# Convolution, projections and attention of a hybrid encoder layer recorded with interleaved priorities, the convolution writing the mix first

## The chip, the cores and the metric

One Trainium2 chip (trn2), all 8 NeuronCores, one launch. Each core handles one new stream of 2048 frames and two running streams of 64 frames; weights are read by every core. The time is device microseconds of the slowest core. Some executions of these kernels fall into a slower state, in which the cores of one die show a lower granted clock (in the changed kernel's one of 2205.4 us, cores 0 to 3 have 0.84 to 0.85, the others 0.97 to 0.98); those runs are left out of every comparison here.

## The reference, cut to what matters

```python
def encoder_layer(x, c, ...):
    x = x + 0.5 * gt1 * swiglu(modulate(rmsnorm(x)), w_ffn1_in, w_ffn1_out)
    h = modulate(rmsnorm(x, g_mix), sh2, sc2)
    z = h @ w_in                                   # q k v f | B C X | gate_attn gate_conv
    logf = log_sigmoid(z_f + b_f)
    o_attn = fox_attention(q, k, v, logf, past_k, past_v, past_logf)   # 16 heads of 64
    o_conv = z_B * short_conv(z_C * z_X, past_u, conv_w)
    m = sigmoid(z_GA) * o_attn + sigmoid(z_GC) * o_conv
    x = x + gt2 * (m @ w_out)
    x = x + 0.5 * gt3 * swiglu(modulate(rmsnorm(x)), w_ffn2_in, w_ffn2_out)
```

Attention and convolution both read `h` and meet only in `m`. Nothing in the reference says which is computed first, nor which of them writes `m` and which adds.

## The kernel before

The kernel records every operation as a node with its buffers and a **priority** (a lower number goes first). A list scheduler inside the program builder then fixes, ahead of time, the order of the instructions on each engine and the slots of the tile pools; semaphores follow from that order. Head pairs are numbered `c` = 0 to 7, position blocks `tb` = 0 to 3 (512 frames) and 4 (the running streams).

```python
p_a = Pool("a", banks[0:4], excl=True)        # PSUM: scores (and FFN)
p_o = Pool("o", banks[4:6], excl=True)        # attention output, output projection
p_p = Pool("p", banks[6:8], excl=True)        # PSUM: projections
...
LOOK = -0.008                                  # scores go ahead of their turn by this
def attend(c):
    ...                                        # per q block, head, key tile of 128:
    mm(scores -> p_a tile, prio=LOOK)          # 1 matmul of up to 512 columns (+ mask)
    act(exp: p_a tile -> pt tile)              # ScalarE, bias from the forget sums
    mm(pt x v -> p_o tile)                     # up to 4 matmuls of 65 columns
    ...
    # gate: t2 * (1 + tanh), transpose through p_p, then
    copy(lambda: (mv(c, tb), pt.ap[:, 0:n // 2].bitcast(BF16)), n, [pt], [MB[c][tb]])   # WRITES the mix
def conv(c):
    for tb, (t0, n) in enumerate(TBS):
        gate = conv_end[-2:-1]                 # wait for the convolution two blocks back
        pc = proj(wC, tb, None, gate); px = proj(wX, tb, None, gate)
        ...                                    # u = C * X; three taps on VectorE (line 1260, 1264)
        pb = proj(wB, tb, None, gate)          # cy = B * cy          (line 1269)
        pg = proj(wG, tb, None, gate)          # cy = cy * (1 + tanh) (line 1274)
        conv_end.append(dve(mv(c, tb) = cy + mv(c, tb)))   # ADDS to the mix (line 1277)
...
for c in range(8):
    P.at(300.0 + c * 10 + 5);  kvqga(c + 1)    # keys, queries, values, attention gate
    P.at(300.0 + c * 10);      attend(c)
    P.at(500.0 + c * 10);      conv(c)         # after everything else of the sub-layer
...
# output projection: residual loads wait for the last convolution
P.dma("sync", xo <- xs, [XS[tb]], [xo], [lastc])
```

`pb` in the profiles is PSUM; `RG`, `RX`, `SC` are SBUF regions, `WS` the weights, `H` the normalised input. So `pb<-H,WS` are projections and feed-forward matmuls, `pb<-WS,H` the projections with positions as rows, `RG<-pb,NF` the exponentials.

The softmax here doesn't subtract the row's maximum and nothing guards it: scores larger than these inputs give would overflow.

Of the kernel before, what the change touches and what calls it, by code (L numbers as in the profile page):

```python
# [15 lines left out]
NT = 2176  # L16
NPR = 2048
# [96 lines left out]
class Node:  # L114
    __slots__ = ("idx", "alts", "deps", "outs", "prio", "dma", "alloc", "tiles", "ndep",
                 "ready", "eng", "start", "fin", "tok", "need", "know", "tbl", "done", "q")


class Prog:
# [19 lines left out]

    def _new(self, reads, writes, after, prio):  # L140
# [11 lines left out]
        n.prio = self.base + self.step * 1e-3 + (prio or 0.0)  # L152
# [243 lines left out]
    def assign(self):  # L396
# [38 lines left out]
        while did < total:  # L435
# [36 lines left out]
            if not moved:  # L472
                for e, o in self.order.items():
                    if ptr[e] < len(o):
                        n = o[ptr[e]]
                        print([(t.pool.name, [m.idx for m in t.nodes]) for t in n.tiles], n.ndep)
                        print(e, ptr[e], n.idx, n.start, n.ready, [(m.idx, m.eng, m.start, m.fin, k) for m, k in n.deps.items() if id(m) not in ready])
# [39 lines left out]
def build_program():  # L517
# [34 lines left out]
    with ExitStack() as ctx:  # L552
# [51 lines left out]
        p_a = Pool("a", banks[0:4], excl=True)  # L604
        p_o = Pool("o", banks[4:6], excl=True)
        p_p = Pool("p", banks[6:8], excl=True)
# [339 lines left out]
        def rgf(off, n):  # L946
# [3 lines left out]
        T1F = rx(BOFF[0], NT)  # L950
        CT16 = rxb(BOFF[0] + 8704, NT)
        ETF = rx(BOFF[1], NT)
        B_t1f, B_ct, B_etf = Buf("t1f", xu[0]), Buf("ct", xu[0]), Buf("etf", xu[1])
        B_ctd = Buf("ctd")

        k_augs = [rg(GB_[0], 2 * NT).rearrange("p (h t) -> p h t", h=2),
                  rxb(BOFF[0], 2 * NT).rearrange("p (h t) -> p h t", h=2)]
        q_augs = [rg(GB_[1], 2 * NT).rearrange("p (h t) -> p h t", h=2),
                  rxb(BOFF[1], 2 * NT).rearrange("p (h t) -> p h t", h=2)]
        VW = 17 * 2 * 66  # L960
        v_exts = [rg(GB_[2], VW).rearrange("p (i h d) -> p i h d", i=17, h=2),
                  rxb(BOFF[0] + 8704, VW).rearrange("p (i h d) -> p i h d", i=17, h=2)]
# [13 lines left out]
        sl_b0 = Slot(rx(BOFF[0] + 13192 + 8, 512), xu[0])  # L976
        sl_b1 = Slot(rx(BOFF[1] + 12928, 512), xu[1])
        a_b0 = Slot(rxb(BOFF[0] + 13192 + 8 + 2048, 512), xu[0])
        a_b1 = Slot(rxb(BOFF[1] + 12928 + 2048, 512), xu[1])
        sl_b4 = [Slot(rx(BOFF[4], 512), xu[4]), Slot(rx(BOFF[4] + 2048, 512), xu[4])]  # L980
        sl_g3 = Slot(rgf(GB_[3] + 8192, 512), gu[3])
        p_sga = Pool("sga", [sl_b0, sl_b1, sslots[0], sslots[1]])
# [6 lines left out]
        p_at = Pool("at", [a_b0, a_b1])  # L989
# [21 lines left out]
        for (o, n, init) in ((0, NPR, None), (NPR, SQ, 0), (NPR + SQ, SQ, 1)):  # L1011
# [12 lines left out]
        fu = B_t1f.users() + B_ct.users()  # L1024
        eu = B_etf.users()
        B_k = [[[Buf("k", gu[0]) for _ in range(5)] for _ in range(2)],
               [[Buf("k", xu[0] + fu) for _ in range(5)] for _ in range(2)]]
        B_krow = [Buf("krow", gu[0]), Buf("krow", xu[0] + fu)]
        B_q = [[[Buf("q", gu[1]) for _ in range(5)] for _ in range(2)],
               [[Buf("q", xu[1] + eu) for _ in range(5)] for _ in range(2)]]  # L1030
        B_qrow = [[Buf("qrow", gu[1]) for _ in range(2)], [Buf("qrow", xu[1] + eu) for _ in range(2)]]
        B_v = [[Buf("v", gu[2]) for _ in range(5)], [Buf("v", xu[0] + fu) for _ in range(5)]]
        B_vone = [Buf("vone", gu[2]), Buf("vone", xu[0] + fu)]
# [34 lines left out]
        sga = {}  # L1068

        def kvqga(c):  # L1070
# [11 lines left out]
            for tb, (t0, n) in enumerate(TBS):  # L1082
# [10 lines left out]
                for hh in range(2):  # L1093
# [14 lines left out]
                sgt = p_sga.tile()  # L1108
                pg, _ = proj_tok(wG, tb, (), [sgt])
                sga[(c, tb)] = sgt  # L1110
                act(lambda sgt=sgt, pg=pg, nt=nt: (sgt.ap[:, 0:nt * 128], pg.ap[:, 0:nt * 128]), AF.Tanh,
                    nt * 128, [pg], [sgt], scale=0.5)
# [7 lines left out]
        LOOK = -0.008  # L1120

        def attend(c):
# [15 lines left out]
            def gate(tb, nsub, t2):  # L1138
                n = nsub * 128
                sgt = sga[(c, tb)]  # L1140
                at = p_at.tile()
                dve(lambda e: e.scalar_tensor_tensor(out=at.ap[:, 0:n], in0=sgt.ap[:, 0:n], scalar=1.0,
                                                     in1=t2.ap[:, 0:n], op0=ALU.add, op1=ALU.mult),
                    n, [sgt, t2], [at])
                pt = p_p.tile()
                tr(lambda: [(pt.ap[:, s * 64:(s + 1) * 64].bitcast(BF16), at.ap[:, s * 128:(s + 1) * 128],
                             ident_bf[:]) for s in range(nsub)], [at, B_const], [pt], [128] * nsub)
                copy(lambda: (mv(c, tb), pt.ap[:, 0:n // 2].bitcast(BF16)), n, [pt], [MB[c][tb]], rate=1.5)

            for qb in range(4):  # L1150
                q0 = qb * 512
                t2 = p_t2.tile()
                for hh in range(2):
# [3 lines left out]
                    for i in range(nt):  # L1157
                        r = i - 4 * qb
                        lo = max(r, 0) * 128
                        s_ = p_a.tile()  # L1160
# [18 lines left out]
                gate(qb, 4, t2)  # L1179

            t2 = p_t2.tile()
            for hh in range(2):
                head = 2 * c + hh
                ot = p_o.tile()
                s_ = p_a.tile()
                mm(lambda s_=s_, hh=hh: [
                    (s_.ap[:, 0:128], ka[0:65, hh, NPR:NT], qa[0:65, hh, NPR:NT], True, False),
                    (s_.ap[:, 0:128], ident_bf[:], mask2[:], False, True)],
                   [B_k[st][hh][4], B_krow[st], B_q[st][hh][4], B_qrow[st][hh], B_const], [s_], [128, 128],
                   prio=LOOK)  # L1190
                pt = p_pt.tile()
                act(lambda pt=pt, s_=s_: (pt.ap[:, 0:128], s_.ap[:, 0:128]), AF.Exp, 128, [s_, B_nf], [pt],
                    bias=NF[:, 256 + head:257 + head], scale=1.0)
                mm(lambda pt=pt, ot=ot, hh=hh: [(ot.ap[:, 0:65], pt.ap[:, 0:128], va[:, 16, hh, 0:65], True, False)],
                   [pt, B_v[st][4], B_vone[st]], [ot], [65], nogroup=True)
                for s in range(2):
                    s_ = p_a.tile()
                    c0 = NPR + s * SQ
                    mm(lambda s_=s_, s=s, hh=hh, c0=c0: [
                        (s_.ap[:, i * 64:(i + 1) * 64], kc_aug[0:65, s, hh, i * 128:(i + 1) * 128],  # L1200
                         qa[0:65, hh, c0:c0 + SQ], True, True) for i in range(8)],
                       [B_kc, B_kcrow, B_q[st][hh][4], B_qrow[st][hh]], [s_], [64] * 8, prio=LOOK)
                    bt = p_t2.tile()
                    dve(lambda e, s_=s_, bt=bt, s=s, head=head: e.tensor_tensor(
                        out=bt.ap[:, 0:512].rearrange("p (i q) -> p i q", i=8),
                        in0=s_.ap[:, 0:512].rearrange("p (i q) -> p i q", i=8),
                        in1=NFS[:, s * 128:(s + 1) * 128].rearrange("p (i h) -> p i h", i=8)[
                            :, :, head:head + 1].to_broadcast([128, 8, 64]), op=ALU.add),
                        512, [s_, B_nfs], [bt])
                    pt = p_pt.tile()  # L1210
                    act(lambda pt=pt, bt=bt: (pt.ap[:, 0:512], bt.ap[:, 0:512]), AF.Exp, 512, [bt], [pt])
                    mm(lambda pt=pt, ot=ot, s=s, hh=hh: [
                        (ot.ap[s * 64:(s + 1) * 64, 0:65], pt.ap[:, i * 64:(i + 1) * 64],
                         vc_ext[:, s, i, hh, 0:65], False, s == 1 and i == 7) for i in range(8)],
                       [pt, B_vc], [ot], [65] * 8, nogroup=True)
                finish(ot, 1, hh, t2)
            gate(4, 1, t2)
# [4 lines left out]
        def conv(c):  # L1222
# [6 lines left out]
            for tb, (t0, n) in enumerate(TBS):  # L1229
                sg = segs(tb)  # L1230
                gate = conv_end[-2:-1]
                pc = proj(wC, tb, None, gate)
                t1 = p_t1.tile()
                copy(lambda t1=t1, pc=pc, n=n: (t1.ap[:, 0:n], pc.ap[:, 0:n]), n, [pc], [t1])
                px = proj(wX, tb, None, gate)
# [31 lines left out]
                pb = proj(wB, tb, None, gate)  # L1267
                for si, (lo, ln_, seq) in enumerate(sg):
# [3 lines left out]
                pg = proj(wG, tb, None, gate)  # L1272
                act(lambda pg=pg, n=n: (pg.ap[:, 0:n], pg.ap[:, 0:n]), AF.Tanh, n, [], [pg], scale=0.5)
                dve(lambda e, pg=pg, cy=cy, n=n: e.scalar_tensor_tensor(
                    out=cy.ap[:, 0:n], in0=pg.ap[:, 0:n], scalar=1.0, in1=cy.ap[:, 0:n],
                    op0=ALU.add, op1=ALU.mult), n, [pg, cy], [cy])
                conv_end.append(dve(lambda e, cy=cy, tb=tb, n=n: e.tensor_tensor(
                    out=mv(c, tb), in0=cy.ap[:, 0:n], in1=mv(c, tb), op=ALU.add), n, [cy, MB[c][tb]], [MB[c][tb]]))

        P.at(300.0)  # L1280
        cache_load(0)
        kvqga(0)
        for c in range(8):
            if c + 1 < 8:
                P.at(300.0 + c * 10 + 5)
                kvqga(c + 1)
            P.at(300.0 + c * 10)
            attend(c)
            if c + 1 < 8:
                P.at(300.0 + c * 10 + 6)  # L1290
# [192 lines left out]
```

## Time and profile before

| | before |
|---|---|
| fast runs, us | 2178.0, 2179.3, 2184.8 (slow state: 2299.6) |
| spans of the cores in the profiled run | 2160.6 to 2179.7 |
| TensorE / ScalarE (ACT) / VectorE (DVE) busy | 89% / 35% / 38% |
| first score matmul to last product with values (core 7) | 667 to 1258 us |
| convolution alone after that | to about 1541 us |

The prediction shows the main lines. One more view belongs with them: the chain that ended last, in order of time, in one position block of the convolution (start, length, what; the small pieces left out).

```profile
1347.63 3.63 PE pb L646 x16
...
1351.42 0.70 DVE RG L1238
...
1353.15 0.76 DVE SC L1264
1354.00 0.76 DVE SC L1264
...
1354.92 0.70 DVE SC L1269
...
1355.76 3.63 PE pb L646 x16
```

From one pair of projections to the next, 8.1 us pass. TensorE is the chain for 3.63 us, VectorE's taps and products for the rest, in part beside TensorE's other pair: with two projection banks, the next projection can't start until line 1269 has read one of them. The profile puts 45.8 us of TensorE's waits from 1268 to 1541 us to that line, in 35 waits (core 0).

### The profile page before, as it was taken

How to read it: one execution, taken by the hardware profiler on the slowest of the kernel's cores; microseconds unless marked ns; L12 is line 12 of the kernel's file. 1: busy time of each engine (PE TensorE's matmuls, PEld its weight loads, DVE VectorE, ACT ScalarE, POOL GpSimd, SP SyncE). 2: the span in 40 equal slices, each digit the busy share in tenths (PEclk: the TensorE clock that was granted, in tenths of full speed). 3: DMA queues.
4: the chain of work that ended last, by engine and by line, in shares of the span. 5: the costliest groups of instructions: out<-in, count | busy, mean ns of one | idle time of the engine just before them, and what ended most of it. 6: DMA issues, size and time to landing. Idle time of an engine off the chain costs nothing.

```text
span 2179.7 us, 38451 instructions; the slowest of 8 cores (2160.6 to 2179.7 us)
## 1 busy us (share of the span) xinstructions
PE 1949.7 (89%) x14273; PEld 1052.6 (48%) x14273; DVE 837.1 (38%) x1592; ACT 755.4 (35%) x1425; POOL 163.1 (7%) x312
## 2 busy tenths in 40 slices
PE   2599999999879999999998988788789999999986
PEld 0245445544336666666666643333334444444433
DVE  0432232223444334433533356666545122322244
ACT  3621101113435576577567630000047110011122
POOL 2101102110011000000000000000000000010000
PEclk7699999999877899999999999999999999999998
DMA  9924506552262222221322211111153221042022
GB/s 237 142 43 68 89 1 95 83 85 64 88 115 63 50 51 64 62 55 48 82 51 53 62 20 20 32 28 20 27 139 78 49 39 20 1 86 36 15 77 87
DMA packets 67460, 137.50 MB, mean 63 GB/s; under 512 B 8416, under 2 KB 12640, under 8 KB 65728
## 3 DMA queue, kind: packets, MB, share of 16 engines
q0 software_dynamic: 41680, 80.92, 23.1%
q1 hardware_dynamic: 25600, 54.12, 7.3%
q8 instruction: 119, 1.95, 0.4%
q14 instruction: 61, 0.50, 0.1%
HBM read 180.04 MB, written 35.89 MB: 99 GB/s over the span
## 4 chain that ended last, share of the span: by engine, by line
PE 74%; DVE 10%; issue 6%; ACT 5%; DMA 4%; DVEq 0%; SPq 0%; ACTq 0%; POOLq 0%; POOL 0%
PE pb L646 74%; ACT RG L668 4%; DVE SC L1264 2%; DMA G<-g 1%; DVE SC L1269 1%; DVE RG L1238 1%; DVE SC L798 1%; ACT H L668 1%; ACT SC L668 1%; DMA BADA<-b_ada 1%; DVE SC L1260 1%; DVE SC L812 1%; DMA WS<-w_ada 0%; DMA yT<-SC 0%; DVE RX L853 0%
## 5 line engine op out<-in xcount | busy, mean ns | idle before, releaser
L646 PE MATMUL pb<-H,WS 128*128 128x512 bf16 (+2 forms) x5480 | 1059.2, 352 | 69.0 <-DVE SC L1269 47.8
L646 PEld LDWEIGHTS pb<-H,WS 128*128 128x128 bf16 (+1 forms) x5480 | 489.4, 99 | 599.9 <-issue 124.6
L646 PE MATMUL pb<-RG,WS 128*128 128x512 bf16 (+1 forms) x1888 | 366.6, 355 | 33.7 <-DVE RX L853 31.3
L668 ACT ACTIVATE SC<-pb 128x512 bf16<-128x512 f32 (+3 forms) x260 | 138.4, 533 | 716.8 <-PE pb L646 710.0
L668 ACT ACTIVATE RG<-pb,NF 128x512 bf16<-128x512 f32 (+3 forms) x656 | 338.6, 792 | 13.0 <-PE pb L646 12.4
L837 DVE TENSOR_TENSOR RG<-pb,SC 128x512 bf16<-128x512 f32 (+1 forms) x220 | 134.5, 612 | 478.0 <-PE pb L646 463.7
L646 PEld LDWEIGHTS pb<-RG,WS 128*128 128x128 bf16 x1888 | 174.6, 101 | 223.4 <-issue 65.3
L853 DVE SCALAR_TENSOR_TENSOR RX<-pb,DER,RX 128x512 f32<-128x512 f32 (+1 forms) x192 | 112.8, 595 | 232.8 <-PE pb L646 229.7
L646 PE MATMUL pb<-RG 128*128 128x65 bf16 (+4 forms) x1424 | 148.5, 236 | 15.8 <-ACT RG L668 4.8
L668 ACT ACTIVATE SC<-RX 128x512 bf16<-128x512 f32 (+1 forms) x160 | 84.8, 559 | 187.0 <-PE pb L646 89.6
L646 PE MATMUL pb<-WS,H 128*128 128x128 bf16 x2176 | 132.9, 222 | 5.3 <-DVE RG L680 4.1
L646 PE MATMUL pb<-RX 65*128 65x512 bf16 (+3 forms) x456 | 116.9, 317 | 18.0 <-ACT RG L668 4.9
L646 PEld LDWEIGHTS pb<-WS,H 128*128 128x128 bf16 x2176 | 126.3, 100 | 13.2 <-issue 11.6
L646 PEld LDWEIGHTS pb<-RG 128*128 128x128 bf16 (+1 forms) x1424 | 87.2, 101 | 66.0 <-issue 42.6
L668 ACT ACTIVATE pb<-pb 128x512 f32<-128x512 f32 (+1 forms) x40 | 20.7, 518 | 268.2 <-PE pb L646 268.2
L646 PE MATMUL pb<-RX,RG 128*128 128x65 bf16 (+1 forms) x1352 | 98.5, 199 | 1.1 <-ACT RG L668 0.8
L646 PEld LDWEIGHTS pb<-RX,RG 128*128 128x128 bf16 (+1 forms) x1352 | 79.4, 104 | 32.2 <-issue 9.4
L668 ACT ACTIVATE H<-SC,MOD 128x512 bf16<-128x512 f32 (+1 forms) x144 | 78.4, 591 | 47.7 <-DVE SC L798 47.6
L798 DVE SCALAR_TENSOR_TENSOR SC<-RX,DER,SC 128x512 f32<-128x512 f32 (+1 forms) x144 | 78.8, 593 | 26.5 <-ACT H L668 18.1
L1128 DVE RECIPROCAL RS<-pb 128x4 f32<-128x4 f32 (+1 forms) x80 | 14.2, 178 | 162.7 <-PE pb L646 161.5
L646 PE MATMUL pb<-SC,ones_bf 128*128 128x512 bf16 (+1 forms) x160 | 50.1, 387 | 29.1 <-ACT SC L668 29.0
L693 POOL DMA_DIRECT2D WS<-w_in x64 | 33.8, 540 | 491.4 <-PE pb L646 488.9
(100 smaller groups left out, 1037.3 us busy)
## 6 DMA issues: line engine op xcount, KB each, us to landing
WS<-w_ada POOLq DMA_DIRECT2D x72, 256.0 KB, 9.9
WS<-w_in POOLq DMA_DIRECT2D x64, 256.0 KB, 5.8
WS<-w1i POOLq DMA_DIRECT2D x44, 256.0 KB, 9.2
WS<-w2i POOLq DMA_DIRECT2D x44, 256.0 KB, 7.3
RX<-xT SPq DMA_DIRECT2D x4, 2048.0 KB
xs<-RX SPq DMA_DIRECT2D x4, 2048.0 KB
kT<-SC SPq DMA_DIRECT2D x32, 256.0 KB
vo<-SC SPq DMA_DIRECT2D x32, 256.0 KB
```

The lines of the kernel that those rows point to most:

```text
L646: ins = e.matmul(o, lhsT=l, rhs=r, start=st, stop=sp, skip_group_check=nogroup)
L668: return e.activation(out=out, in_=in_, func=func, **kw)
L693: P.dma("gpsimd", lambda e: e.dma_start(out=t.ap[:, 0:n], in_=src), 128 * n * 4, (), [t], after, prio)
L798: dve(lambda e, k=k, tm=tm, lo=lo, ln_=ln_, seq=seq: e.scalar_tensor_tensor(out=tm.ap[:, lo:lo + ln_], in0=xap(k, tb, lo, ln_), scalar=der ...
L812: dve(lambda e, k=k, tm=tm: e.scalar_tensor_tensor(out=tm.ap[:, 0:n], in0=xap(k, tb), scalar=g3v[:, 3, k, 0:1], in1=rs.ap[:, 0:n], op0=ALU ...
L837: dve(lambda e, n=n, tb=tb, jj=jj, sa=sa, pb=pb: e.tensor_tensor(out=gap(jj, tb), in0=pb.ap[:, 0:n], in1=sa.ap[:, 0:n // 2].bitcast(BF16), ...
L853: dve(lambda e, tb=tb, mo=mo, po=po, lo=lo, ln_=ln_, seq=seq: e.scalar_tensor_tensor(out=xap(mo, tb, lo, ln_), in0=po.ap[:, lo:lo + ln_], ...
L1128: dve(lambda e: e.reciprocal(out=rc.ap[:, 0:nsub], in_=ot.ap[:, 0:nsub * 66].rearrange("p (s d) -> p s d", s=nsub)[:, :, 64]), nsub, [ot], ...
L1238: dve(lambda e, u=u, px=px, t1=t1, lo=lo, ln_=ln_, si=si: e.tensor_tensor(out=u.ap[:, lo + 2 + 2 * si:lo + 2 + 2 * si + ln_], in0=px.ap[:, ...
L1260: dve(lambda e, u=u, cy=cy, m=m: e.tensor_scalar(out=cy.ap[:, 0:m], in0=u.ap[:, 0:m], scalar1=CW[:, c * 3:c * 3 + 1], scalar2=None, op0=AL ...
L1264: dve(lambda e, u=u, cy=cy, m=m, j=j: e.scalar_tensor_tensor(out=cy.ap[:, 0:m], in0=u.ap[:, j:j + m], scalar=CW[:, c * 3 + j:c * 3 + j + 1 ...
L1269: dve(lambda e, pb=pb, cy=cy, lo=lo, ln_=ln_, si=si: e.tensor_tensor(out=cy.ap[:, lo:lo + ln_], in0=pb.ap[:, lo:lo + ln_], in1=cy.ap[:, lo ...
```

## The change

Its intent: let the convolution run beside attention, so that TensorE always has projections to do while ScalarE works on exponentials. For that the convolution writes the mix and attention adds to it; the gate projection of attention moves into attention; priorities are spread over each piece in proportion to its TensorE time. Cut to its core:

```diff
+    def spread(self, first, lo, hi):           # priorities by TensorE share
+        ns = self.nodes[first:]
+        tot = sum(n.alts["tensor"][1] for n in ns if "tensor" in n.alts) or 1.0
+        acc = 0.0
+        for n in ns:
+            n.prio = lo + (hi - lo) * acc / tot + n.extra
+            if "tensor" in n.alts:
+                acc += n.alts["tensor"][1]
...
+        p_s = Pool("s", banks[0:3], excl=True)            # scores: 3 banks for 4
-        p_p = Pool("p", banks[6:8], excl=True)
+        p_p = Pool("p", [banks[3]] + banks[6:8], excl=True)   # projections: 3 for 2
...
-        LOOK = -0.008
+        LOOK = -0.03
...          attention's gate
-                copy(lambda: (mv(c, tb), pt...bitcast(BF16)), n, [pt], [MB[c][tb]], rate=1.5)
+                dve(lambda e: e.tensor_tensor(out=mv(c, tb), in0=pt..., in1=mv(c, tb), op=ALU.add), ...)
...          convolution: no `gate`, and one VectorE operation less
-                dve(... cy = (pg + 1) * cy ...)
-                conv_end.append(dve(... mv(c, tb) = cy + mv(c, tb) ...))
+                conv_end.append(dve(... mv(c, tb) = (pg + 1) * cy ...))
...          order
-            P.at(300.0 + c * 10 + 5); kvqga(c + 1)
-            P.at(300.0 + c * 10);     attend(c)
-            P.at(500.0 + c * 10);     conv(c)
+            lastk = spread(kvq, c, V0 + c - 1.0, V0 + c - 0.1)
+            spread(conv, c, V0 + c - 0.75, V0 + c + 0.2)
+            spread(attend, c, V0 + c, V0 + c + 1)          # gate projection inside
...          output projection: residual loads
-                    128 * n * 4, [XS[tb]], [xo], [lastc])
+                    128 * n * 4, [XS[tb]], [xo], [lastk])
```

Left out: the sample streams' attention moves to the middle of `attend`, the first head pair's buffers change places with the second's, two small pools fall away, the residual loads have three buffers for four. `LOOK` counts in other units in the two kernels (single steps of the recording before, shares of a head pair's work after), so its two values can't be compared directly.

## The prediction

> **What bounds the kernel now.** I read the spans of the eight cores first: 2160.6 to 2179.7 us in the profiled execution, so no core is an outlier, and the two fast timed runs are 2179.3 and 2184.8 (the third, 2299.6, is the slow state). Then the page of the slowest core:
>
> ```profile
> PE 1949.7 (89%) x14273; PEld 1052.6 (48%) x14273; DVE 837.1 (38%) x1592; ACT 755.4 (35%) x1425; POOL 163.1 (7%) x312
> PE   2599999999879999999998988788789999999986
> ACT  3621101113435576577567630000047110011122
> PEclk7699999999877899999999999999999999999998
> ```
>
> TensorE looks 89% busy, but ends of matmuls are modelled, so that row hides waits. The ACT row is the telling one: high for slices 12 to 24, zero for slices 25 to 29. Two halves of the mixing sub-layer stand one after the other: attention (much ACT) and then the convolution (no ACT). I cut the span at these borders and asked for each stretch:
>
> ```profile
> core 0: us, PE busy (x) PEld busy (x) DVE busy (x) ACT busy (x) POOL busy (x), PEclk, DMA share, GB/s
> 540.00:650.00 110.00, 87.09 (x397) 39.16 (x395) 49.66 (x93) 44.62 (x83) 7.59 (x15) 0.79 0.42 97
> 650.00:1268.00 618.00, 570.82 (x6594) 392.16 (x6593) 244.84 (x494) 412.47 (x793) 28.30 (x49) 0.94 0.25 57
> 1268.00:1541.00 273.00, 222.47 (x1137) 100.90 (x1135) 179.79 (x374) 21.25 (x44) 12.67 (x24) 0.97 0.14 24
> 1541.00:1672.00 131.00, 110.75 (x566) 51.63 (x566) 73.66 (x129) 58.62 (x94) 5.19 (x10) 0.96 0.31 85
> 1672.00:2090.00 418.00, 417.40 (x2254) 202.39 (x2255) 104.45 (x182) 71.43 (x142) 29.68 (x57) 1.00 0.22 37
> ```
>
> The last row is a feed-forward stretch and gives the yardstick. Its matmuls are 1804 of 512 columns and 440 of 128, which start 216 and 56 ns apart: 1804 x 0.216 + 440 x 0.056 = 414 of 418 us. So dense TensorE work loses 1%. The same count (starts read from the trace, 65-column matmuls 30 ns apart, 384 and 256 columns 162 and 109) for the others:
> - 650 to 1268, attention with projections: 2176 x 0.056 + 514 x 0.216 = 233 for projections; 448 x 0.216 + 64 x 0.162 + 64 x 0.109 = 114 for scores, 2192 x 0.030 = 66 for weights times values, some 52 for masks, transposes and the cached streams. Sum 465 of 618 us: 153 lost.
> - 1268 to 1541, convolution: 904 x 0.216 + 224 x 0.056 = 208 of 273: 65 lost.
> - 1541 to 1672, output projection: 106 at these spacings, 25 lost. 540 to 650: 83, 27 lost.
>
> What the waits are:
>
> ```profile
> 854.67 16.23 ACT L668 ACTIVATE RG<-pb,NF 128x512 bf16<-128x512 f32 x30
> ```
> ```profile
> L668 ACT ACTIVATE RG<-pb,NF 128x512 bf16<-128x512 f32 x448 | 273.7, 879 | 2.4 <-PE pb L646 1.8
> ```
> ```profile
> PE pb L646 <- DVE SC L1269: 45.8, 35, 2.5
> ```
> ```profile
> 1355.76 6.42 PE L646 MATMUL pb<-H,WS 128*128 128x512 bf16 x29 [1.07 <-DVE SC L1269]
> ```
>
> First line, ACT in the last third of one head pair's attention: 30 exponentials back to back, no gap, 0.54 us each (a full one starts 0.57 after the last). TensorE's share of a full tile is 0.216 + 4 x 0.030 = 0.34 us. With no other matmuls left at that point, ACT is the bound. Second: one exponential lasts 0.88 us from start to end[...]. Third and fourth, from the convolution: TensorE waits some 1 us per position block, 35 times, for the VectorE product that frees a PSUM bank.
>
> [...]cores 0 and 1 record 0.8125 from about 575 to 735 us, the other six do not[...].
>
> **The change part by part.**
> 1. *Removed:* the convolution's last add into the mix. 32 x 0.692 + 8 x 0.293 = 24 us of DVE. The gate's copy out of PSUM (24 DVE at 0.425, some on ACT at 0.58, small ones) becomes an add: 24 us for 17. DVE and ACT together save about 17 us, in stretches where neither is full: nothing directly. What counts is the order: the convolution no longer waits for attention's result, so it can run before it.
> 2. *Moved:* the order of the built program shows it. Cut into pieces of 25 us of TensorE work, the old order has pieces with 21 us of projections, then pieces with 22 us of attention, then eight pieces of convolution alone. The new one has, from the first score tile on, about 7.7 attention, 8.6 convolution, 8.7 projections in every piece for 600 us. No matmul is added: both programs hold the same TensorE work.
> 3. *Distance:* TensorE work between a score matmul and the product that needs its exponential: median 1.24 us before, 2.73 after; 347 of 688 products have less than the needed 1.25 before, 67 after, most at the end of the last head pair.
> 4. *Banks:* scores keep 3 banks of 4, projections get 3 for 2. Three score tiles per 1.4 us round trip is 0.47 us each, shorter than an exponential: no bound.
> 5. *ACT in the mix:* exponentials 448 x 0.569 + 64 x 0.463 + 64 x 0.356 + 80 x 0.25 = 327, cached streams 17, tanh 36, and copies (97 now on ACT by the new order, 69 before) about 43: 423 us in some 700, 60%. DVE about 390, 56%. Both below TensorE.
> 6. *Ends:* the first head's convolution fills the wait for the cumulative forget sums (chain at 656 to 665 us), worth a few us; the residual loads of the output projection no longer wait for the convolution, worth perhaps 5. The last head pair has no projections and soon no convolution beside it: 20 us of exponentials against 11 of TensorE, about 10 us lost.
>
> Sum for 650 to 1541 (891 us): floor 465 + 208 = 673. Attention's loss scaled by the short distances, 153 x 67/347 = 30. For the convolution's bank waits I take a quarter of 65, 16: a third bank and other matmuls between. That is 719, a gain of 172. Ends: some 3 more. 2184.8 - 175 = 2010.
>
> **The rivals.**
> - *ACT or DVE order becomes the wait.* The order on each engine is fixed ahead of time[...]. For: twice as many switches of kind (2380 runs of equal matmuls against 1947), 79 projection copies now among the exponentials, one score bank less. Against: 1.5 us slack over the need, and the old stretches that have projections beside attention are already dense. If half of the old loss stays: 891 - 110 gives about 2075.
> - *The clock.* If 1500 us without rest bring the 0.8125 of cores 0 and 1 back, for example over 300 us, that costs 300 x (1/0.8125 - 1) = 69: about 2080. For: it appeared right after 464 dense us. Against: six cores did not have it, and 440 to 505 dense us in the second feed-forward part have it nowhere.
> - *All of it gained*, [...]floor 2184.8 - (153 + 65 + 20) = 1947. Cores' clock of 0.94 in attention speaks for some of it.
> - *Weight loads late*, since gate weights are held through attention: eight slots hold two sets, and DMA is at 25%; I give it little.
>
> **Range and chances.** 2010; the first two rivals together set the upper end at 2085, the third the lower at 1955. Even half the gain is over 5%, so faster by 2%: 0.95; within: 0.04; slower: 0.01.
>
> **What would show it.** Right: the ACT row at 5 to 7 through the whole mixing stage and no slices of zero; the stage from the first score to the last product about 700 us long; no run of exponentials without gaps except in its last 30 us; TensorE waits for L1269's successor a few us. The prediction is wrong if TensorE waits in the mix for exponentials or bank readers add to over 100 us, if the clock row falls to 8 there, or if the gain of the middle is given back in the output projection.

Its sum: 673 + 30 + 16 = 719 of 891 us, a gain of 172, with 3 for the ends 175, so 2184.8 - 175 = 2010. "The needed 1.25" is the time in us from the end of a score matmul's issue to the product with its exponential; it was partly the author's estimate, and the 30 rests on it. The trace of core 7 before gives nearly the same: 0.20 from the end of a score matmul's issue to the exponential's start and 0.14 from its end to the product (medians of waits) make 1.22 with the 0.88, and 1.44, the "round trip", with the 0.216 of the matmul itself. That the busy row hides waits can be read from the records: one of 512 columns lasts 387 to 394 ns on core 0, and dense ones start 216 ns apart. In the first rival, that late VectorE copies hold TensorE had no measurement behind it. In the third, the 20 us in the floor were the author's estimate for half-speed spells; the clock records before do show such spells, but not what sets them off.

## The result, and the profile after

The changed kernel took 1982.7, 1983.7 and 1985.3 us in its fast runs (one slow run of 2205.4), median of all four 1984.5; before, 2182.0. The ratio is 0.910, with a 95% interval of 0.907 to 0.912. Ratios here and below are the mean time of one kernel's fast runs over that of the other's of the same rounds, so not quite the ratio of the medians quoted. Executions in which one die ran at a lower clock are left out of the means. Results are correct. Later the same two kernels gave 1985.2 and 2175.3, 0.913.

The page of the slowest core after (busy times, then 40 equal slices of the span in tenths):

```profile
PE 1850.1 (93%) x14273; PEld 1012.9 (51%) x14273; DVE 783.5 (39%) x1524; ACT 794.9 (40%) x1455; POOL 163.1 (8%) x312
PE   2499999999987999999999999998999999999986
ACT  3541100111343366666666766668573110111122
PEclk9999999999997999999999999998999999999998
```

The ACT row no longer has a hole: it is at 6 or more from slice 15 on and falls only where attention ends. The clock row stays at 9 through the whole mix. The stretches, cut at the new borders, with the same columns as before:

```profile
650.00:695.00 45.00, 40.55 (x286) 21.89 (x284) 28.17 (x39) 10.38 (x20) 5.45 (x6) 0.92 0.27 61
695.00:1325.00 630.00, 623.15 (x6855) 402.06 (x6854) 338.04 (x739) 409.82 (x755) 35.01 (x66) 1.00 0.31 61
1325.00:1389.00 64.00, 57.03 (x672) 38.87 (x668) 20.53 (x57) 49.03 (x93) 4.76 (x9) 0.92 0.30 51
1389.00:1480.00 91.00, 87.10 (x449) 41.27 (x450) 52.33 (x87) 55.09 (x88) 0.95 (x2) 0.98 0.32 90
1480.00:1895.00 415.00, 414.61 (x2249) 201.22 (x2248) 106.16 (x186) 75.62 (x145) 29.67 (x57) 1.00 0.25 38
```

The second row is the mix: 630 us with a granted clock of 1.00 on all eight cores, and TensorE shown busy but for 7 us. The list of what TensorE waited for there, in all (us, times, longest):

```profile
PE pb L657 <- ACT SC L679: 2.7, 14, 0.4
PE pb L657 <- ACT RG L679: 1.6, 7, 0.5
```

This list shows only a part: the record of a 512-column matmul lasts 0.38 us on average here (core 7), and dense ones start 0.216 apart, so the records cover waits. In the old attention, where the prediction counts 153 us lost, its largest entry for TensorE was no more than this (core 0, 650 to 1268 us):

```profile
PE pb L646 <- ACT RG L668: 10.7, 49, 0.5
```

Counted by the starts of matmuls, as below, the 630 us lose 22, not 4. Some 19 of these lie in steps over 60 ns longer than the dense spacing; the semaphores put 5 of them to exponentials, 5 to copies on ACT, 2 to VectorE, and for 7 they name nobody. By the same count the old attention of core 7 lost 145 us, of which 84 are put to exponentials.

And ACT in the last head pair's attention, where nothing is left to mix in:

```profile
1369.58 16.84 ACT L679 ACTIVATE RG<-pb,NF 128x512 bf16<-128x512 f32 x31
```

This is the old picture, 31 exponentials without a gap, once instead of eight times.

To say where the time came from, I count matmuls times their dense spacing in each stretch, as in the prediction, and call the rest lost. Core 7 has a complete record in both traces and no stretch at 0.8125 of the clock:

| core 7, from 650 us on | before: us (lost) | after: us (lost) |
|---|---|---|
| to the first score matmul | 17 (6) | 45 (9) |
| first score to last product | 591 (146) | 693 (43.5) |
| from there to the end | 912 (123) | 596 (37) |
| - of which convolution alone | (65) | none |
| - output projection, to dense feed-forward | (30) | (6) |
| - the rest, mostly the final norm | (28) | (31) |
| sum lost | 275 | 90 |

The difference, some 186 us, is that of the two spans (2170.5 and 1983.8). The count is good to about 1 us per stretch, depending on the spacing taken for the smallest matmuls. Of the 43.5 us, 22 lie in the mix and 21 in the last 64 us, where attention stands alone. Below, "the mix" in such counts is the whole stretch from the first score to the last product.

### The profile page after: what moved, and what is told of

It reads as the page before. It is cut to its first block, busy times and chain, and to the rows that moved or that the text cites. A ratio compares the mean times of both kernels' runs of the same rounds, so it can differ in the third digit from the quotient of the medians.

```text
span 1983.8 us, 38303 instructions; the slowest of 8 cores (1978.3 to 1983.8 us)
## 1 busy us (share of the span) xinstructions
PE 1850.1 (93%) x14273; PEld 1012.9 (51%) x14273; DVE 783.5 (39%) x1524; ACT 794.9 (40%) x1455; POOL 163.1 (8%) x312
## 4 chain that ended last, share of the span: by engine, by line
PE 86%; DMA 4%; DVE 4%; issue 3%; ACT 3%; POOL 0%; DVEq 0%; SPq 0%; ACTq 0%; POOLq 0%
PE pb L657 85%; DMA WS<-w_ada 3%; ACT RG L679 1%; ACT SC L679 1%; DVE SC L809 1%; ACT H L679 1%; DVE SC L823 1%; DMA yT<-SC 1%; DVE RX L864 0%; PE pb L665 0%; DVE RG L1287 0%; DVE RG L1018 0%; DVE RX L691 0%; DVE RG L1014 0%; DVE SC L1132 0%
## 5 line engine op out<-in xcount | busy, mean ns | idle before, releaser
L657 PE MATMUL pb<-H,WS 128*128 128x512 bf16 (+2 forms) x5480 | 1084.7, 349 | 15.3 <-DVE RX L691 5.8
L657 PEld LDWEIGHTS pb<-H,WS 128*128 128x128 bf16 (+1 forms) x5480 | 482.2, 98 | 491.7 <-issue 33.6
L679 ACT ACTIVATE SC<-pb 128x512 bf16<-128x512 f32 (+3 forms) x280 | 148.9, 532 | 683.9 <-PE pb L657 673.2
L679 ACT ACTIVATE RG<-pb,NF 128x512 bf16<-128x512 f32 (+3 forms) x656 | 367.0, 618 | 124.0 <-PE pb L657 122.5
L657 PE MATMUL pb<-RG 128*128 128x65 bf16 (+4 forms) x1424 | 143.0, 232 | 6.5 <-ACT RG L679 3.1
L657 PE MATMUL pb<-WS,H 128*128 128x128 bf16 x2176 | 145.7, 220 | 0.0
L679 ACT ACTIVATE H<-SC,MOD 128x512 bf16<-128x512 f32 (+1 forms) x144 | 78.3, 591 | 43.5 <-DVE SC L809 43.4
L657 PEld LDWEIGHTS pb<-RX,RG 128*128 128x128 bf16 (+1 forms) x1352 | 74.0, 100 | 41.8 <-issue 6.2
L657 PE MATMUL pb<-RX,RG 128*128 128x65 bf16 (+1 forms) x1352 | 93.1, 194 | 0.0
L1277 DVE SCALAR_TENSOR_TENSOR SC<-RG,CW,SC 128x512 f32<-128x512 f32 (+1 forms) x80 | 53.7, 671 | 8.0 <-DVE SC L1277 0.5
L657 PE MATMUL pb<-CSB,WS 128*128 128x3 bf16 x576 | 19.9, 165 | 37.5 <-DMA WS<-w_ada 35.8
```

The costliest lines, as they stand in the source:

```text
L657: ins = e.matmul(o, lhsT=l, rhs=r, start=st, stop=sp, skip_group_check=nogroup)
L679: return e.activation(out=out, in_=in_, func=func, **kw)
L1277: dve(lambda e, u=u, cy=cy, m=m, j=j: e.scalar_tensor_tensor(out=cy.ap[:, 0:m], in0=u.ap[:, j:j + m], scalar=CW[:, c * 3 + j:c * 3 + j + 1 ...
```

## The experiments

The changed kernel's fast runs were 1982.7 to 1985.8 us, which is the mark for the first eight experiments. They were run at other times. Differences of a few us from it are no firmer than that. The last three ran beside it.

**e1_conv_first.** All convolutions first, then attention with projections, everything else as changed.

```diff
-            spread(conv, c, V0 + c - 0.75, V0 + c + 0.2)
+            spread(conv, c, V0 - 9.0 + c, V0 - 8.0 + c)
```

> The changed kernel with one edit: all eight convolutions get a priority ahead of the projections and attention, so they run alone first; attention still adds to the mix and keeps its spread with the projections. Tests whether the gain is the mixing in time, or the other parts of the change (fewer VectorE adds, third projection bank, dependency turned round), which all stay. Theory (mixing): attention with projections alone needs about 22 us of ACT per 25 us of TensorE work, close to ACT's limit, and half of the score-to-product distances shrink (median 1.87 us for 2.73), so that stretch loses 40 to 80 us more; the convolution alone with three banks loses 10 to 40 more. About 2045 us (2020 to 2090). Rival (the other parts are the gain): within 10 us of 1984.

Measured: 2034.0 us, ratio 0.935 to before: 50 slower than the change, 142 faster than before. The theory holds, and its split can be read from the stretches (core 7: the convolution alone, then attention with projections):

```profile
660.00:900.00 240.00, 223.89 (x1267) 110.07 (x1268) 169.39 (x363) 23.99 (x52) 18.23 (x31) 1.00 0.19 30
912.00:1448.00 536.00, 511.00 (x6500) 359.96 (x6499) 233.77 (x495) 416.37 (x780) 24.47 (x46) 0.99 0.32 70
```

Attention takes 536 us for a count of 464, so 72 are lost, half of the old 146: here the projections lie evenly beside attention, instead of in lumps before each head pair. No run separates that from what else changed in this stretch, the longer lookahead above all (median distance 1.87 us for 1.24). The stretch from 650 us to the first score, which holds the convolution, loses 23, where the old convolution lost 65; it has the third bank and lacks the old gate. So mixing the *convolution* into attention is worth 50 of the 197 us; most of the gain is there without it.

**e2_attn_writes.** The old write order, but interleaved: each convolution one unit later.

```diff
-                dve(... mv(c, tb) = pt + mv(c, tb) ...)
+                copy(lambda: (mv(c, tb), pt...), n, [pt], [MB[c][tb]], rate=1.5)
...              convolution again with cy = (pg + 1) * cy, then mv = cy + mv
-            spread(conv, c, V0 + c - 0.75, V0 + c + 0.2)
             spread(attend, c, V0 + c, V0 + c + 1)
+            spread(conv, c, V0 + c + 0.25, V0 + c + 1.2)
```

> The changed kernel with the write order of before: attention writes the mix, the convolution adds to it with its own VectorE add, and each convolution stands one unit later, so it still runs beside attention of the next heads. Tests whether turning the write order round is needed or only lets the convolution run early. Theory (mixing is the gain): the last 20 to 30 us of convolution now fill the last attention, which was left alone with ACT, and 17 us of VectorE work come back off the path: 1970 to 1995 us. Rival (the removed VectorE work and waits are the gain): 2040 or more.

Measured: 1979.1 us, ratio 0.910 (0.908 to 0.912). The same as the change within the intervals. On core 7 the last convolution does fill the last attention (the mix loses 26 us), but the output projection then waits for it (19 lost for 6). Turning the write order round is not what brings the gain: with the convolution lagging by one head pair, the old order interleaves as well. The VectorE work that the change saved had no effect that these runs can show.

**e4_short_look.** The lookahead of the scores cut.

```diff
-        LOOK = -0.03
+        LOOK = -0.01
```

> The changed kernel with the lookahead of the score matmuls cut from 0.03 to 0.01 of a head pair's priority unit: the share of each engine's work in time stays the same, but the median TensorE work between a score matmul and the product that needs it falls from 2.73 to 1.41 us and 195 products (67 before) have less than the needed 1.25. Theory A (distance matters as much as the mixing): shortfall sums to 57 us in the order for 17, so about 40 us slower, 2015 to 2040. Theory B (the share of work is what counts; TensorE is only held by exponentials when ACT is full): within 15 us of 1984.

Measured: 1996.8 us, ratio 0.918 (0.917 to 0.919). 12 slower: theory B is nearer, but the distance is not free. The mix lost 55 us for 43.5. The 40 us that I had taken from the summed shortfall were an estimate, too many by a factor of three; why is not shown.

**e5_gate_in_kvq.** The gate projection back among the others.

```diff
-        p_sga = Pool("sga", sslots[0:2])
+        p_sga = Pool("sga", [sl_b0, sl_b1, sslots[0], sslots[1]])
...              in kvq, per position block
+                sgt = p_sga.tile()
+                pg, _ = proj_tok(wG, tb, (), [sgt])
+                wga[(c, tb)] = sgt
+                act(... tanh: pg -> sgt ...)
...              gate_in(tb) in attend
+                return wga[(c, tb)]
...              output projection: two more waits for the buffers' last users
```

> The changed kernel with the gate projection back among the key, query and value projections (four sigmoid buffers as before, in the space the change left free), all else the same. Tests that part of the change. Theory: the same matmuls and tanh in a slightly different place, so within 10 us of 1984; if the gate projection inside attention is an essential filler, or frees buffers that held TensorE, 20 us or more slower.

Measured: 1975.1 us, ratio 0.908. As expected within 10 us, and on the fast side: this part of the change is not a gain, rather a loss: some 9 us, 4 by the ratios to before (0.908 and 0.910). The wait for the first score lost 3 us for 9 on core 7, since the first head pair's gate projections now fill it, and the mix 39 for 43.5. e12 repeats it beside the changed kernel.

**e6_before_banks.** The kernel before with the change's PSUM split alone.

```diff
+        p_s = Pool("s", banks[0:3], excl=True)     # used for the scores
-        p_p = Pool("p", banks[6:8], excl=True)
+        p_p = Pool("p", [banks[3]] + banks[6:8], excl=True)
```

> The kernel before with only the change's split of PSUM banks: scores 3 banks for 4, projections 3 for 2; order, writes and lookahead as before. Theory (mixing is the gain): the third projection bank helps the convolution stretch by some of its 65 lost us, but the third score bank's absence shortens the distance from score to product (median 0.85 us for 1.24; 612 products under 1.25 us for 347), so attention gets slower by as much or more: between 20 faster and 40 slower than before. Rival (the bank split is a large part of the gain): 50 us or more faster than before.

Measured: fast runs 2151.7, 2152.7 and 2162.0 us, ratio 0.991 (0.987 to 0.995): some 20 faster than before, at the edge of the range. Both halves of the expectation happened, on core 7 first before (attention, convolution), then with the split:

```profile
667.00:1258.00 591.00, 543.55 (x6403) 372.60 (x6399) 227.44 (x477) 403.37 (x779) 24.44 (x46) 0.96 0.25 57
1258.00:1541.00 283.00, 232.29 (x1184) 105.34 (x1183) 186.90 (x386) 21.84 (x45) 12.66 (x24) 0.98 0.15 23
```
```profile
666.00:1285.00 619.00, 585.40 (x6321) 402.08 (x6319) 220.96 (x459) 423.62 (x792) 24.49 (x46) 0.83 0.24 54
1285.00:1535.00 250.00, 232.17 (x1263) 111.28 (x1259) 180.20 (x385) 35.95 (x71) 12.70 (x24) 1.00 0.16 26
```

The convolution loses 21 us by count, for 65: its waits were bank waits, as the chain said. Attention got 28 us longer (180 lost for 146), and its granted clock fell from 0.96 to 0.83: half-speed spells add up to 212 us in this stretch on this core, against 48 before. In both kernels the row "PE busy" grows with the slower clock, one more reason not to read it as work. The bank split alone is thus no good trade; beside interleaving, it costs nothing that the trace shows. The reverse, the change with the old 4 and 2 banks, does not build, with or without the old gate in the convolution: this scheduler stops with no order found, most of what is left waiting for a projection bank. So with this scheduler the third bank is also what makes this interleaving possible.

**e7_tail.** The convolutions spread thinner, so that the last one accompanies the last attention.

```diff
-            spread(conv, c, V0 + c - 0.75, V0 + c + 0.2)
+            spread(conv, c, V0 - 0.75 + 1.07 * c, V0 - 0.75 + 1.07 * (c + 1))
```

> The changed kernel with the eight convolutions spread 7% thinner, so that the last one lies beside the last head pair's attention almost to its end instead of ending a fifth into it. Tests the loss I put at about 10 us for the last attention, which has exponentials and little else. Theory: 8 to 15 us faster than 1984 (shortfall in the order 6 us for 17); if the last attention is bounded by something else, within 4 us.

Measured: 1981.2, 1999.1 and 2005.2 us (and a slow run of 2057.1). This is inconclusive as a time. In the two longer runs, two cores that are neighbours were slow and the other six were not (the profiled one, spans and granted clocks):

```profile
core 4: 1997.5 us, clock 0.955
core 5: 1997.0 us, clock 0.958
core 6: 1972.3 us, clock 0.970
core 7: 1975.2 us, clock 0.969
```

The records of cores 4 and 5 show 0.8125 of the clock for 159 us from about 670 us on. The undisturbed cores of these two runs are at 1972 to 1978 us, some 5 less than the 1977 to 1984 of the changed kernel: less than I expected, as the mix lost 40 us for 43.5.

**e8_before_half_exp** and **e9_after_half_exp.** Both kernels: less work per exponential, the same order on every engine. The outputs were wrong (relative error 0.14 and 0.15).

```diff
-  (pt.ap[:, lo:512], s_.ap[:, lo:512]), AF.Exp
+  (pt.ap[:, lo:min(512, lo + 256)], s_.ap[:, lo:min(512, lo + 256)]), AF.Exp
```

> The kernel before, wrong on purpose: each exponential works on at most 256 of its columns, the rest of the tile is stale. Order of every engine the same. It takes 448 x (0.569 - 0.356) + 64 x (0.463 - 0.356) = 102 us of ACT work out. Theory (old attention is bounded by ACT where no projections are left, else by the exponential's latency): 60 to 110 us faster than before, all of it between 650 and 1268 us. Rival (ACT is not on the path; TensorE's own order, semaphores or banks hold it): under 20 us faster.

> The changed kernel with the same cut in the exponentials, wrong on purpose. Theory: with the mixing ACT is off the path except beside the last head pair, so 10 to 25 us faster than 1984, nearly all at the end of the last attention. Rival (attention in the mix still waits for ACT): 40 us or more.

Measured: e8 2090.9 us, 86 faster than before by the medians (ratio 0.963, which makes 81: one of its four fast runs took 2107); e9 1971.2 us, 13 to 14 faster than the change (ratio 0.906). Both as the theory has it. The attention stretch of e8:

```profile
650.00:1175.00 525.00, 494.00 (x6504) 358.17 (x6542) 239.56 (x490) 307.97 (x790) 28.29 (x49) 1.00 0.30 66
```

It is 525 us for the 618 of the old kernel, at a clock of 1.00 (the slowest core of each; on core 7, from first score to last product, 506 for 591). The 86 us hold what the clock gained: on core 7 the old attention has 48 us at half speed, this one none. The mix of e9, then its last attention:

```profile
695.00:1325.00 630.00, 624.88 (x6883) 403.41 (x6881) 339.51 (x743) 327.36 (x756) 35.01 (x66) 1.00 0.31 61
1325.00:1372.00 47.00, 44.49 (x629) 32.17 (x627) 18.16 (x52) 36.16 (x93) 4.76 (x9) 1.00 0.38 66
```

In the mix, 82 us less of ACT (409.8 to 327.4) change next to nothing: in the same 630 us nearly the same matmuls (6883 for 6855), and 20 us lost for 22. In the last attention, 64 us become 47. The same cut is worth over 80 us in the old order and next to nothing where something lies beside the exponentials. It shortens each exponential and ACT's whole load at once, so it doesn't say which of the two held TensorE before.

**e10_before_early_loads** and **e11_after_late_loads.** The gate of the residual loads, changed alone in each kernel.

```diff
# e10, in the kernel before (lastk: the last value projection)
-                    128 * n * 4, [XS[tb]], [xo], [lastc])
+                    128 * n * 4, [XS[tb]], [xo], [lastk])
# e11, in the changed kernel (lastm: the last attention add)
-                    128 * n * 4, [XS[tb]], [xo], [lastk])
+                    128 * n * 4, [XS[tb]], [xo], [lastm])
```

> The kernel before with one edit: the residual loads of the output projection wait for the last value projection, not for the last convolution, as in the change. Stretch sums show that the stretch from the end of the mix to dense feed-forward work lost 32 us before and 12 after, where I had put 5 for these loads. Theory (the loads are that gain): 10 to 20 us faster than before. Rival (the gain there comes from output projection blocks running while attention still finishes): within 6 us of before.

> The changed kernel with the residual loads waiting for the last attention add of the whole mix, so that they come after the sub-layer as they did before. Theory (the loads are the gain of the output projection stretch): 8 to 20 us slower than the changed kernel of the same call. Rival (overlap of blocks, not loads): under 5 us slower.

Measured: e10 2161.8 us, ratio 0.994 (0.993 to 0.995), 13.6 faster than before; e11 1993.0 us against 1985.2 of the changed kernel (0.916 and 0.913 of before), 8 slower. Both lie in the theory's ranges, e11 at the edge. In the waits of the output projection (core 0), first before, then e10, VectorE's wait for the loads and TensorE's for VectorE shrink:

```profile
PE pb L646 <- DVE RX L1344: 14.3, 4, 7.7
DVE RX L1344 <- DMA SC<-xs: 12.5, 7, 3.7
```
```profile
PE pb L646 <- DVE RX L1345: 8.5, 3, 5.9
DVE RX L1345 <- DMA SC<-xs: 7.2, 2, 5.4
```

So the loads are worth 8 to 14 of the 24 us that the output projection lost less. (The 12 in the expectation does not come out of the trace of the changed kernel: from the last product on, 91 us hold 85 us of dense matmuls, 6 lost.) The rest stays open. That output projection blocks run before attention ends, the expectation's rival, can be little of it: on core 7 the first starts 2 us before the last product.

**e12_gate_tail.** e5 and e7 together.

> The gate projection back among the other projections (e5) and the convolutions spread thinner (e7) together, as a version that may beat the change. Products with less than 1.25 us between score and use: 16 for 67. Theory: the 4 to 9 us of each add up, 8 to 14 us faster than the changed kernel of the same call on cores at full clock. If both fill the same hole beside the last head pair, no more than the 6 to 9 us of one.

Measured: 1974.5 us, ratio 0.908 (0.907 to 0.909), against 1985.2 and 0.913 (0.911 to 0.914): 10.7 faster than the change, and the best beside e5 (1975.1). That lies in the range of the theory, that the two gains add up. But e5 alone had nearly the same time, and the mix loses 37.5 us, not the 43.5 minus both gains, which speaks for the same holes. The runs do not settle it. No core's mean granted clock was below 0.967 in the four runs.

**after_again.** The changed kernel unedited, for the comparisons above.

> The changed kernel itself, unedited, so that the runs of this call have it on the same chip. 1980 to 1987 us, 0.906 to 0.912 of before.

Measured: 1983.3 to 1985.8 us fast (one slow run, 2310.1), ratio 0.913, just outside the expected ratios.

## Why the prediction was right, point by point

**Direction and mechanism.** 2010 was predicted, with 1955 to 2085 as the range; 1984.5 was measured. The reading that attention was held by its exponentials is shown by e8 and e9, the reading that the convolution was held by banks by e6. That interleaving fills both is shown in part only: e1 leaves the convolution unmixed and is already 142 us faster than before. In it attention loses 72 us for 146 and the stretch with the convolution 23. So the mixing of the convolution is shown for 50 us. The rest of the gain in the middle comes with the even spread of the projections, the longer lookahead and the third bank; e6 shows the bank's part in the convolution, and no run separates the other two. And part 1 of the prediction says that what counts is the turned order of writing; e2 has the old one and is as fast.

**The middle.** The sum had 30 us left over from attention and 16 from the convolution, 46 in all. The mix lost 43.5. The total is right; how it was put together is not all shown, so that it fits is in part luck. The scaling by short distances (153 x 67/347) was too steep a use of that count: e4 has 195 short products, by that scaling 86 us, and lost 55. The need of 1.25 us was itself too long: its 0.88 us is the record of an exponential that queues behind others. One that doesn't lasts 0.67 to 0.69 us (core 7 before), which makes about 1.0 (an estimate: 0.20 from the end of a score matmul's issue to the exponential's start and 0.14 from its end to the product, both medians of waits on core 7 before). And one reading does not come out: for 540 to 650 us the prediction has 83 us of matmuls and 27 lost, but the trace of core 0 has 291 matmuls of 512 columns and 104 of 128 there, 69 us, 41 lost. Its sum does not use them.

**The ends.** This is the term that was too small. I allowed "some 3 more", made of a few us at the start, 5 for the loads and 10 lost in the last attention. Measured: the start lost 3 more, not less; the output projection lost 24 less, of which the loads are 8 to 14; the final stretch lost 3 more; the last attention's loss is in the 43.5 (21 in its 64 us, of which 8 in the last 19, for which the prediction had 10). So the ends are worth some 18 us. The remaining difference between 175 and 197 is about 10 us of the time before: its first runs, at 2178 to 2185 us, had cores that took longer than core 7 (later 2172 to 2179 for the same kernel).

**The rivals.** Queue order: the mix loses 22 us by count, of which 5 are put to copies on ACT and 2 to VectorE, far from the half of the old loss that this rival meant. The clock: no core of the changed kernel recorded 0.8125 in the profiled run, though e7 shows that a nearly equal kernel can meet it, at 20 us. "All of it gained", 1947, was too much: 43.5 us stay lost, half of them in the last attention. Late weight loads did not show up.

**What the prediction gave too little weight.** Half-speed spells, which it has only as a rival, were a part of the old loss: after the first 100 us they sum to 74 to 154 us per core before and 64 to 73 after. And the gate projection inside attention, which I took for neutral, costs some 4 to 9 us (e5; e12 has it together with e7).

## What to carry to other kernels

Where one stretch is full on ScalarE and the next on TensorE, compare the dense time of TensorE's matmuls with the length of each stretch; the difference can be filled by laying the stretches side by side, and a cut of the suspected cost in both kernels (e8, e9) shows whether it was the bound and still is. Here an even spread of what was already beside attention and a longer lookahead, with one more bank for the projections, gave most of the gain; mixing in the next piece gave the last quarter (e1). Look at the ends of a newly merged stretch as well: loads that waited for the old last step, and the last block that has nothing beside it.

## What these runs show of the clock and of ScalarE

- Granted clock: all eight cores of the changed kernel ran the 630 us mix and then 415 us of feed-forward at a mean of 1.00 in the profiled run. On core 0 before, matmuls of 512 columns start 216 ns apart (median) where the clock record shows 1.0, 263 where it shows 0.8125 and 427 where it shows 0.5. Where 0.8125 was recorded in a profiled fast run, it held two neighbouring cores (0 and 1 before, 128 and 143 us in all; 4 and 5 in e7, 159 us), and cost e7 about 20 us. In the slow runs the four cores of one die go down together, to means of 0.79 to 0.95, but no trace of a slow run was kept. What sets either off stays open.
- Half speed: in the attention of before, core 7 has 48 us at half speed, though no two matmuls in a row started more than 0.8 us apart there. With 180 of 619 us of attention lost (e6) the granted clock was 0.83, with 146 of 591 (before) 0.96, with 72 of 536 (e1) 0.99, all on core 7. The runs do not show what sets the spells off.
- ScalarE: exponentials of 512 columns start 569 to 570 ns apart when they queue (core 7 before). The record of each grows when they do: on core 0 before, from 0.68 us on average for the first of a row to 0.94 from the ninth on, 879 ns over all (688 on core 7 after). So sums of recorded durations overstate ACT.
